# A decoder step on one core: weight sums moved beside the scores, left factors ordered and pooled anew

## The chip, the cores and the metric

The program runs on one core of a Trainium2 chip. The metric is the device time of one launch in microseconds, the median over several runs; lower is better. The core has five engines that each work through their own list of instructions in order: TensorE (PE in the profile; PEld is its weight load), VectorE (DVE), ScalarE (ACT), GpSimd (POOL) and SyncE (SP). In this kernel SP issues every DMA.

## The reference

One layer of a decoder for 2048 prompt tokens and 64 sample tokens, width 1024, all in fp32: a mixer of mLSTM heads and a convolution module, cross-attention into 256 memory tokens, then a ConvFFN. Cut to the parts that the change touches:

```python
qx = (hc @ w['x_wq']).reshape(B, L, X_HEADS, X_HEAD_DIM)
sc = jnp.einsum('blhd,bmhd->bhlm', qx, mem_k) * (X_HEAD_DIM ** -0.5)     # scores
pr = jax.nn.softmax(sc, axis=-1)
ox = jnp.einsum('bhlm,bmhd->blhd', pr, mem_v).reshape(B, L, D_MODEL)
x = x + ox @ w['x_wo']                                                   # output rows
hf = rmsnorm(x, w['norm_ffn'])
uf = hf @ w['f_wup']                                                     # (tokens,1024)@(1024,5632)
fa, fg = uf[..., :D_FF], uf[..., D_FF:]
fa_c = causal_dwconv(f_ext, w['f_conv_w'], w['f_conv_b'])                # width 3
x = x + (jax.nn.gelu(fa_c) * fg) @ w['f_wdown']                          # (tokens,2816)@(2816,1024)
y = rmsnorm(x, norm_final)
```

## The kernel before, in words

Every fp32 operand of a product is split into a high part (an ACT cast to fp32r) and a low part (a DVE or POOL subtraction): `split`. A product is then three matmuls: `mm3`. The large products are taken as 2 by 2 blocks with seven products in place of eight, named B11, B21, B22, T1, T2, T3, T4. Each needs a left and a right factor, which are blocks or sums of blocks.

The stages that matter here, by their place in the span: the *folds* (to 990 us) multiply `x_wq` into the memory keys and so make seven sets of right factors. `put` splits some tiles of them straight into `wf0` to `wf6`; the rest goes to DRAM (`wfd`) and comes back through `load_factors`. *Scores* (991 to 1186): eight pairs of 128-row token tiles. A pair is loaded and normed (`pair_in`), transposed and summed to left factors (`pair_sums`: four POOL sums `a<-a` among them), and split into seven left tiles `l` (`pair_split`); then come the seven products. Two of the seven left tiles lie in pool `pa`; the other five lie in `ap`, a pool that opens once the fold pool `fms` is closed, in the same space. *Output rows* (1186 to 1425) do the same with the probabilities and with seven factor sets `mo`.

*FFN up* (1441 to 2426): three blocks of 6, 5 and 5 token tiles. `rows_in` loads and norms a block's rows in two halves, `block_input` transposes them and makes seven right operands `R0` to `R6`, and 11 steps over weight pairs follow (`raw<-in_f_wup`, sums, splits into `wt`). The first block's rows are loaded, both halves, before `block_input` is entered. The left factors of the next stage are stored to DRAM as `l_d`.

*Down-projection* (2441 to 2899): for each of the seven products (B11, B21, T2, T3, T1, B22, T4) eleven right tiles `ws` (`wt` or `w`) and eight left factors, j = 0 to 7: `left_factor` loads `lr` (704 KB), splits it into `l` and 33 matmuls run, one unit. The residual rows `acc` are loaded beside the first two products. `weight_sums(k)`, once for each k of 11, is called beside units 1 to 11: it loads two tiles of `f_wdown` (`wr`, 512 KB each), multiplies them with the sample rows (`psG<-wr,ysr`), makes the four sums, two on DVE and two on POOL, and stores them as `ds`, from where the right factors T1 to T4 are read back.

All of `xt`, `raw` (of factor sets), `wr` and the probabilities share one ring of six tiles (pool `xw`). A scheduler sets each engine's order from the program order and its estimates.

Of the kernel before, what the change touches and what calls it, by code (L numbers as in the profile page):

```python
# [45 lines left out]
L_BUFS = 2, 6  # L46
# [42 lines left out]
R_ORDER = 1, 2, 3, 0, 4, 5, 6  # L89
# [4 lines left out]
def trunk_kernel(ctx: ExitStack, tc: tile.TileContext, i: dict, o: list):  # L94
# [1002 lines left out]
    def fold_keys(pools, mT, ps_, tps_):  # L1097
# [363 lines left out]
    def rows_in(blk, junk=None):  # L1461

        t0, nt_, smp = blk
        hc = nt_ * P // 2
        halves = []
        for z in range(2):
            xts = []
            first, n = t0 * P + z * hc, hc + (HS if smp else 0)
            for c0 in range(0, n, P):
                nt = min(P, n - c0)  # L1470
                t = xw.tile([P, D], F32, name="xt", tag="xt")
                c = c0
                while c < c0 + nt:
                    if c < hc:
                        tid, r0 = divmod(first + c, P)
                        m = min(P - r0, c0 + nt - c, hc - c)
                    else:
                        tid, r0, m = NT, z * HS, HS
                    SY.dma_start(t[c - c0:c - c0 + m], x2_d[tid][r0:r0 + m])
                    c += m  # L1480
                norm_x([(t, nt)], junk() if junk else fe_.tile([P, D], BF16, name="junk", tag="junk"), V)
                xts.append((t, nt))
            halves.append(xts)
        return halves
# [126 lines left out]

    pas = ExitStack()
# [97 lines left out]
    def block_input(blk, rows):  # L1710
# [118 lines left out]
    wdn = i["f_wdown"][0]  # L1829
# [7 lines left out]
    R_next = block_input(C_BLOCKS[0], ahead)  # L1837
    for bi, (t0, nt_, smp) in enumerate(C_BLOCKS):
# [84 lines left out]
    lp = ctx.enter_context(tc.tile_pool(name="lp", bufs=2, side="right", reuse_waits="tile"))  # L1923
# [35 lines left out]

    sums_d = [[dram(f"ds{kh}_{k}", [P, 2, 512]) for k in range(FP)] for kh in range(2)]  # L1960
# [4 lines left out]
    def weight_sums(k):  # L1965

        r = []
        for kh in range(2):
            t = xw.tile([P, 2, 512], F32, name="wr", tag="xt")
            SY.dma_start(t, wdn[(2 * k + kh) * P:(2 * k + kh + 1) * P, :].rearrange("p (c d) -> p c d", c=2))  # L1970
            for c in range(2):
                mm(pts[c * S:(c + 1) * S], ysr[:, 2 * k + kh], t[:, c], k + kh == 0, k + kh == FP)
            r.append(t)
        (b11, b12), (b21, b22) = [[t[:, c] for c in range(2)] for t in r]
        tt(b22, b22, b12, ALU.subtract)
        tt(b12, b12, b11, ALU.subtract, G)
        tt(b11, b11, b22, ALU.add)
# [126 lines left out]
```

## Time and profile before

| | |
|---|---|
| runs | 2911.03, 2922.74 (median), 2926.61 us |
| profiled execution | 2908.07 us, its span 2906.3 us |
| PE busy | 2721.0 us, 94% |
| DVE / ACT / POOL busy | 70% / 48% / 41% |
| DMA | 520.39 MB, mean 179 GB/s |

Busy time is the time in which an engine executed; PEclk is the granted clock of TensorE as a share of full speed (1.00 is 2.4 GHz). The span is the profiled execution from its first to its last instruction; 1.8 us of the execution's time lie outside it.

### The profile page before, as it was taken

What the parts mean: (1) busy time and instruction counts of PE and PEld (TensorE: products, weight loads), DVE (VectorE), ACT (ScalarE), POOL (GpSimd) and SP (SyncE); (2) the same over time, 40 slices, a digit from 0 to 9 for tenths busy, and PEclk for the clock granted to TensorE, in tenths of its full rate; (3) what the DMA queues carried; (4) which work ended last, traced back from release to release, by engine and by line L of the source; (5) the groups of instructions that cost most, each with busy time, mean ns of one, the idle gap of its engine ahead of it and who ended that gap; (6) DMA issues with size and microseconds to landing.
All of it is one profiled execution on the core that took longest, in us unless ns stands there. A gap on an engine that the chain in (4) does not pass through costs nothing. (4 is left out here: it accounts for less than half of the span.)

```text
span 2906.3 us, 44255 instructions
## 1 busy us (share of the span) xinstructions
PE 2721.0 (94%) x15768; PEld 2395.9 (82%) x15768; DVE 2042.0 (70%) x3395; ACT 1397.4 (48%) x2777; POOL 1195.4 (41%) x1285
## 2 busy tenths in 40 slices
PE   7999999989989799999799999999999997999998
PEld 6889989976768688666689988899989996678887
DVE  4588898793234678653599999888888885454454
ACT  4576678783232475412463334744454452232233
POOL 1558555461210442533464544554464442213200
PEclk9999999998999899999899999999999998999999
DMA  7635423354576632757645555666656567994454
GB/s 187 198 116 184 129 77 112 107 167 157 181 235 229 228 102 98 243 203 257 201 141 187 169 183 172 179 200 196 197 171 189 169 187 214 329 297 134 135 169 132
DMA packets 433317, 520.39 MB, mean 179 GB/s; under 512 B 61917, under 2 KB 331971, under 8 KB 433088
## 3 DMA queue, kind: packets, MB, share of 16 engines
q1 hardware_dynamic: 433096, 517.56, 56.0%
q8 instruction: 124, 2.03, 0.3%
q14 instruction: 97, 0.79, 0.1%
HBM read 352.18 MB, written 165.65 MB: 178 GB/s over the span
## 5 line engine op out<-in xcount | busy, mean ns | idle before, releaser
L294 ACT CAST wt<-raw 128x512 fp32r<-128x512 f32 x510 | 306.1, 617 | 309.9 <-DVE raw L125 68.4
L125 DVE TENSOR_TENSOR wt<-raw,wt 128x512 fp32r<-128x512 f32 x358 | 321.2, 902 | 45.8 <-ACT wt L294 45.2
L125 POOL TENSOR_TENSOR cside<-cside,cprod 128x512 f32<-128x512 f32 (+2 forms) x248 | 250.4, 1010 | 121.1 <-ACT cprod L117 91.1
L125 POOL TENSOR_TENSOR wt<-raw,wt 128x512 fp32r<-128x512 f32 x152 | 226.0, 1488 | 131.4 <-ACT wt L294 125.7
L122 DVE SCALAR_TENSOR_TENSOR psG<-ue,vc,psG 128x512 f32<-128x512 f32 (+2 forms) x448 | 256.5, 572 | 22.2 <-ACT psG L117 13.3
L148 PE MATMUL psA<-R,wt 128*128 128x384 f32 (+2 forms) x1392 | 246.3, 328 | 5.4 <-DVE u L125 2.6
L148 PEld LDWEIGHTS psA<-R,wt 128*128 128x128 f32 x1392 | 229.4, 191 | 8.1 <-ACT wt L294 3.2
L294 ACT CAST l<-lr 128x1408 fp32r<-128x1408 f32 x56 | 77.0, 1376 | 283.3 <-PE psA L148 67.7
L117 ACT ACTIVATE cprod<-ue,vc 128x512 f32<-128x512 f32 (+2 forms) x248 | 146.6, 604 | 28.2 <-POOL cside L125 20.3
L125 DVE TENSOR_TENSOR l<-lr,l 128x1408 fp32r<-128x1408 f32 x56 | 98.6, 1761 | 67.0 <-ACT l L294 59.3
L122 DVE SCALAR_TENSOR_TENSOR y<-fe,vc,y 128x640 f32<-128x640 f32 (+1 forms) x132 | 134.5, 1052 | 5.4 <-ACT y L117 5.3
L148 PE MATMUL psA<-wf,l 128*128 128x512 f32 x516 | 132.7, 400 | 4.9 <-DVE b L129 1.9
L148 PE MATMUL psG<-R,wt 128*128 128x320 f32 (+2 forms) x696 | 128.3, 327 | 4.6 <-DVE fe L125 2.5
L148 PE MATMUL psD<-R,wt 128*128 128x320 f32 (+2 forms) x696 | 127.8, 328 | 4.8 <-DVE u L125 3.4
L125 POOL TENSOR_TENSOR y<-y,u 128x384 f32<-128x384 f32 (+2 forms) x66 | 80.4, 1218 | 125.5 <-ACT wt L294 51.7
L148 PE MATMUL psE<-R,wt 128*128 128x352 f32 (+2 forms) x696 | 126.3, 324 | 5.7 <-DVE u L125 4.5
L148 PE MATMUL psF<-R,wt 128*128 128x352 f32 (+2 forms) x696 | 126.6, 325 | 3.0 <-DVE fe L125 2.2
L148 PE MATMUL psC<-R,wt 128*128 128x384 f32 (+2 forms) x684 | 121.9, 323 | 7.7 <-DVE u L125 7.7
L148 PE MATMUL psB<-R,wt 128*128 128x384 f32 (+2 forms) x684 | 124.2, 326 | 1.7 <-DVE fe L125 1.5
L148 PE MATMUL psD<-h,wt 128*128 128x256 f32 (+1 forms) x768 | 117.6, 298 | 7.0 <-DMA h<-h 5.3
L141 POOL TENSOR_TENSOR r<-v,nhalf 128x1 f32<-128x1 f32 (+1 forms) x63 | 40.0, 640 | 203.5 <-DVE v L131 201.1
L148 PEld LDWEIGHTS psD<-R,wt 128*128 128x128 f32 x696 | 115.0, 191 | 8.2 <-ACT wt L294 3.2
(662 smaller groups left out, 6934.0 us busy)
## 6 DMA issues: line engine op xcount, KB each, us to landing
raw<-in_f_wup SPq DMA_DIRECT2D x88, 512.0 KB
raw<-sum SPq DMA_DIRECT2D x88, 512.0 KB
lr<-l SPq DMA_DIRECT2D x49, 704.0 KB
sum<-raw SPq DMA_DIRECT2D x44, 512.0 KB
xt<-x SPq DMA_DIRECT2D x42, 512.0 KB
xt<-in_x_prompt SPq DMA_DIRECT2D x32, 512.0 KB
x<-xt SPq DMA_DIRECT2D x32, 512.0 KB
h<-h SPq DMA_DIRECT2D x56, 256.0 KB
```

The source lines that it names most:

```text
L117: A.activation(out, in_, func, bias=bias, scale=scale)
L122: V.scalar_tensor_tensor(out=out, in0=in0, scalar=s, in1=in1, op0=op0, op1=op1)
L125: (eng or V).tensor_tensor(out=out, in0=a, in1=b, op=op)
L141: G.tensor_tensor(out=y, in0=v, in1=e.to_broadcast(sh), op=ALU.pow)
L148: T.matmul(out, lhsT, rhs, start=start, stop=stop)
L294: A.copy(hi, src)
```

## The change

Four edits. (1) `weight_sums` is called beside the scores (pairs 0 to 7) and the output rows (pairs 0 to 2), with all four sums on POOL; the sample rows' product reads `f_wdown` again, a tile for each of 22 units from B21 on (`sample_rows`), and its result is added after T3. (2) Scores: six left tiles lie in a new pool `pl`, and the sixth factor set lies in `ap` beside the seventh left tile; T4's factor tiles all go through DRAM. (3) FFN up: the first block's second half of rows is loaded inside `block_input`; the `R` tiles are allocated in another order, the weight `raw` tiles have a pool of their own, the carry tiles come later. (4) Down: the raw left factors of units 0 and 1 are loaded early into the `xw` ring, unit 0's is split into three `wt` tiles, each later one is loaded two units ahead, and the second half of `acc` is placed beside T2.

```diff
-L_BUFS = 2, 6
+L_BUFS = 6, 2
+ACC_AT = 0, 2
+WF_ORDER = 1, 2, 5, 4, 3, 0
...
-            if dst is None:
+            if dst is None or q == T4:
                 SY.dma_start(wf_d[q][:, k], x)
...
+    def weight_sums(k):
+        r = []
+        for kh in range(2):
+            t = xw.tile([P, 2, 512], F32, name="wr", tag="xt")
+            SY.dma_start(t, wdn[(2 * k + kh) * P:(2 * k + kh + 1) * P, :].rearrange("p (c d) -> p c d", c=2))
+            r.append(t)
+        (b11, b12), (b21, b22) = [[t[:, c] for c in range(2)] for t in r]
+        tt(b22, b22, b12, ALU.subtract, G)
+        tt(b12, b12, b11, ALU.subtract, G)
+        tt(b11, b11, b22, ALU.add, G)
+        tt(b21, b21, b11, ALU.subtract, G)
+        for kh in range(2):
+            SY.dma_start(sums_d[kh][k], r[kh])
...
     nxt += pair_split(sums0, range(L_BUFS[0], 7))
+    wf.append(factor_6())
+    load_factor(wf[6], wf_d[6], KT // 2)
...
             scores(scp, p, left, lambda: next(side) if p + 1 == NT // 2 else None)
+            weight_sums(p)
...
+            if p < FP - NT // 2:
+                weight_sums(NT // 2 + p)
...
-    ahead = rows_in(C_BLOCKS[0], junk_rows)
+    ahead = rows_in(C_BLOCKS[0], 0, junk_rows)
...
+        xts1 = rows[1] if len(rows) > 1 else rows_in(blk, 1, lambda: junk)
...
+    def sample_rows(f):
+        t = xw.tile([P, 2, 512], F32, name="ws", tag="xt")
+        SY.dma_start(t, wdn[f * P:(f + 1) * P, :].rearrange("p (c d) -> p c d", c=2))
+        for c in range(2):
+            mm(pts[c * S:(c + 1) * S], ysr[:, f], t[:, c], f == 0, f == FT - 1)
...
+    with tc.high_priority():
+        ahead = [left_raw(B11, j, True) for j in range(2)]
+    first = left_first(ahead.pop(0))
...
-            l = left_factor(q, j)
-            if qi < 2:
-                accs[qi].append(acc_rows(qi, j))
+            l = left_factor(ahead.pop(0)) if qi + j else first
+            n_ = qi * NJ + j + 2
+            if n_ < len(ORDER) * NJ:
+                ahead.append(left_raw(ORDER[n_ // NJ], n_ % NJ))
+            if qi in ACC_AT:
+                accs[ACC_AT.index(qi)].append(acc_rows(ACC_AT.index(qi), j))
...
-            if qi < 2 and 0 < qi * NJ + j <= FP:
-                weight_sums(qi * NJ + j - 1)
+            if 0 <= (qi - 1) * NJ + j < FT:
+                sample_rows((qi - 1) * NJ + j)
```

Where the order moves, first SP's at the start of the scores. `wfd` are factor tiles in DRAM (the number ending in 40 is T4), `xt<-x` the rows of the pairs, `ds` the weight sums, `p` the probabilities. Before:

```order
L1658 DMA raw<-wfd_10040 128x1024 [waits DMAHW7_49,DVE_49]
L1658 DMA raw<-wfd_10040 128x512 [waits DMAHW6_49,Pool_49]
L1425 DMA xt<-x_2_171 128x1024 [waits DMAHW1_49,DVE_49]
L1425 DMA xt<-x_3_172 128x1024 [waits DMAHW3_49,DVE_49]
L1425 DMA xt<-x_4_173 128x1024 [waits DMAHW0_49,Pool_49]
L1425 DMA xt<-x_5_174 128x1024 [waits DMAHW5_49,DVE_49]
L1425 DMA xt<-x_6_175 128x1024 [waits DMAHW2_49,Pool_49]
L1425 DMA xt<-x_7_176 128x1024 [waits DMAHW4_49,Pool_49]
L1425 DMA xt<-x_8_177 128x1024 [waits DVE_49,PE_49]
L1437 DMA p_10041<-sc 128x512 [waits DVE_49]
```

After:

```order
L1685 DMA raw<-wfd_10040 128x1024 [waits DMAHW4_49,Pool_49]
L1130 DMA wfd_10040<-b 128x512 [waits Pool_49]
L1685 DMA raw<-wfd_10040 128x1024 [waits DMAHW6_49,DMAHW5_49]
L1427 DMA xt<-x_2_171 128x1024 [waits DMAHW1_49,DVE_49]
L1427 DMA xt<-x_3_172 128x1024 [waits DMAHW0_49]
L1619 DMA wr<-in_f_wdown 128x1024 [waits DMAHW2_49,DVE_49,Activation_49]
L1619 DMA wr<-in_f_wdown 128x1024 [waits DMAHW3_49,DVE_49]
L1427 DMA xt<-x_4_173 128x1024 [waits DMAHW4_49,DVE_49,Pool_49]
L1427 DMA xt<-x_5_174 128x1024 [waits DMAHW6_49,DVE_49,Pool_49]
L1619 DMA wr<-in_f_wdown 128x1024 [waits DVE_49,PE_49]
L1439 DMA p_10041<-sc 128x512 [waits DVE_49]
L1627 DMA ds_0_10057<-wr 128x1024 [waits DMAHW7_49,DMAHW1_49,Pool_49]
```

T4's last tile is now written and read back ahead of pair 1's rows, and between the rows of one pair and the next stand the `wr` loads and `ds` stores, the latter behind a wait for POOL.

Next ACT's order at the start of FFN up. `b<-psB` is the first transposed feature of the block, `junk,ss<-xt` and `xt<-xt,r` are a row tile's squares and its scaling. Before:

```order
L294 CAST wt<-raw 128x512 [waits PE_49]
L294 CAST wt<-raw 128x512 [waits DVE_49]
L294 CAST wt<-raw 128x512 [waits Pool_49]
L294 CAST wt<-raw 128x512 x2
L294 CAST wt<-raw 128x512 [waits DMAHW3_49]
L294 CAST wt<-raw 128x512 [waits DMAHW6_49]
L294 CAST wt<-raw 128x512
L119 ACTIVATE junk,ss<-xt 128x1024 [waits DMAHW7_49]
L117 ACTIVATE xt<-xt,r 128x1024 [waits DMAHW4_49,Activation_49,Pool_49]
L119 ACTIVATE junk,ss<-xt 128x1024 [waits DMAHW2_49]
L117 ACTIVATE b<-psB,vc_432 128x384
L117 ACTIVATE b<-psC,vc_432 128x384
```

After:

```order
L296 CAST wt<-raw 128x512 [waits DMAHW7_49]
L296 CAST wt<-raw 128x512
L119 ACTIVATE b<-psB,vc_432 128x384 [waits PE_49]
L119 ACTIVATE b<-psC,vc_432 128x384 [waits PE_49]
L121 ACTIVATE junk,ss<-xt 128x1024 [waits DMAHW6_49,PE_49]
L296 CAST R_15523<-b 128x384 [waits Activation_49] x2
L119 ACTIVATE b<-psB,vc_432 128x384 [waits PE_49]
L119 ACTIVATE b<-psC,vc_432 128x384 [waits PE_49]
L296 CAST wt<-raw 128x512 [waits DVE_49]
L296 CAST wt<-raw 128x512 [waits Pool_49]
L296 CAST wt<-raw 128x512 x2
L296 CAST wt<-raw 128x512 [waits DMAHW0_49]
```

The first features now stand behind two weight casts, not behind eight casts and two tiles' squares and scaling; the other casts follow two features later.

Last SP's order at the start of the down-projection, from the last store of the stage ahead (`l<-ls`). `lr<-l` are raw left factors, of rows of 128 or 64 tokens. Before:

```order
L1905 DMA l_15367<-ls 128x4x320 [waits DMAHW0_49,Pool_49]
L2003 DMA lr<-l_15365 128x11x128 [waits DMAHW1_49]
L1955 DMA acc<-x_0_186 128x1024 [waits DMAHW2_49,PE_49]
L2056 DMA ysr<-ys 128x1408 [waits DMAHW7_49,DMAHW5_49,DMAHW3_49]
L2059 DMA accs<-x_16_202 64x512 [waits DMAHW4_49]
L2059 DMA accs<-x_16_202 64x512
L2003 DMA lr<-l_15365 128x11x128 [waits DMAHW6_49]
L1955 DMA acc<-x_1_187 128x1024 [waits PE_49]
L1955 DMA acc<-x_2_188 128x1024 [waits DMAHW0_49]
L1955 DMA acc<-x_6_192 128x1024 [waits DMAHW1_49]
L1970 DMA wr<-in_f_wdown 128x1024 [waits DMAHW2_49,DVE_49]
L1955 DMA acc<-x_7_193 128x1024 [waits DMAHW3_49]
```

After, from the same store, and then the piece that ends with unit 5's factor (two halves of 64 rows):

```order
L1939 DMA l_15473<-ls 128x4x320 [waits DMAHW6_49,Pool_49]
L2030 DMA lr<-l_15471 128x11x128 [waits DMAHW7_49,PE_49]
L1989 DMA acc<-x_0_186 128x1024 [waits DMAHW0_49,PE_49]
L2109 DMA ysr<-ys 128x1408 [waits DMAHW5_49,DMAHW3_49,DMAHW1_49]
L2112 DMA accs<-x_16_202 64x512 [waits DMAHW2_49]
L2112 DMA accs<-x_16_202 64x512
L2030 DMA lr<-l_15472 128x11x128 [waits DMAHW4_49]
L1989 DMA acc<-x_1_187 128x1024
L1989 DMA acc<-x_2_188 128x1024 [waits DMAHW6_49]
L1989 DMA acc<-x_6_192 128x1024 [waits DMAHW7_49]
L1989 DMA acc<-x_7_193 128x1024 [waits DMAHW0_49]
L1989 DMA acc<-x_8_194 64x1024 [waits DMAHW1_49]
```

```order
L2015 DMA wr<-in_f_wdown 128x512 [waits DMAHW1_49]
L2000 DMA ws<-in_f_wdown 128x1024 [waits DMAHW2_49]
L1989 DMA acc<-x_3_189 128x1024 [waits DMAHW3_49]
L1989 DMA acc<-x_4_190 128x1024 [waits DMAHW4_49]
L1989 DMA acc<-x_5_191 128x1024 [waits DMAHW5_49]
L1989 DMA acc<-x_8_194 64x1024 [waits DMAHW6_49]
L1989 DMA acc<-x_9_195 64x1024 [waits DMAHW7_49]
L1989 DMA acc<-x_9_195 64x1024 [waits DMAHW0_49,PE_49]
L2030 DMA lr<-l_15472 128x11x64 [waits DMAHW1_49,DVE_49]
L2030 DMA lr<-l_15473 128x11x64 [waits DMAHW2_49]
```

The loads for units 0 and 1 have moved some 170 rows ahead of this place, so the first `lr` here is unit 2's. Unit 4's load stands four rows behind the first of these two pieces, and 19 other loads stand between it and unit 5's.

## Rows read from the trace of the kernel before

**Rows 1.** The page's first part: busy time, share of the span, instructions of each engine.

```profile
PE 2721.0 (94%) x15768; PEld 2395.9 (82%) x15768; DVE 2042.0 (70%) x3395; ACT 1397.4 (48%) x2777; POOL 1195.4 (41%) x1285
```

**Rows 2.** Windows: from:to, length, busy time (instructions) by engine, PEclk, DMA share, GB/s.

```profile
980.00:1017.00 37.00, 18.15 (x104) 15.41 (x103) 31.55 (x32) 23.82 (x44) 29.31 (x24) 0.77 0.65 216
1017.00:1190.00 173.00, 170.41 (x809) 137.89 (x807) 135.67 (x277) 111.13 (x271) 54.07 (x56) 0.99 0.34 112
1190.00:1425.00 235.00, 230.34 (x1218) 159.91 (x1216) 115.61 (x164) 70.55 (x128) 104.17 (x94) 1.00 0.66 232
1425.00:1475.00 50.00, 28.39 (x123) 22.99 (x123) 35.54 (x54) 34.86 (x64) 25.75 (x28) 0.73 0.61 189
1475.00:1805.00 330.00, 306.77 (x1728) 301.16 (x1728) 322.66 (x398) 134.82 (x219) 169.43 (x153) 0.99 0.53 173
2426.50:2600.00 173.50, 153.74 (x623) 106.93 (x621) 77.67 (x92) 45.00 (x55) 37.68 (x26) 0.93 0.99 311
2600.00:2870.00 270.00, 270.00 (x1193) 223.58 (x1192) 137.26 (x147) 84.94 (x101) 51.74 (x35) 1.00 0.54 157
```

**Rows 3.** PE's waits from 930 to 1480: total, times, longest, in us.

```profile
PE psB L145 <- ACT b L117: 17.9, 2, 16.5
PE psG L148 <- ACT l L294: 16.6, 1, 16.6
```

**Rows 4.** PE in order of time, scores' start: start, us, operation [idle before <- releaser].

```profile
994.54 3.01 PE L148 MATMUL psA<-wf,l 128*128 128x512 f32 x12 [0.38 <-DVE b L129]
1014.12 1.22 PE L148 MATMUL psG<-wf,l 128*128 128x512 f32 x2 [16.57 <-ACT l L294]
...
1034.64 2.88 PE L148 MATMUL psG<-wf,l 128*128 128x512 f32 x12
```

**Rows 5.** ACT in order of time at the start of FFN up.

```profile
1425.06 0.62 ACT L294 CAST wt<-raw 128x512 fp32r<-128x512 f32 x1 [4.40 <-PE psA L148]
1432.15 3.73 ACT L294 CAST wt<-raw 128x512 fp32r<-128x512 f32 x7 [6.48 <-DVE raw L125]
1435.94 1.06 ACT L119 ACTIVATE junk<-xt 128x1024 bf16<-128x1024 f32 x1
...
1439.87 1.04 ACT L119 ACTIVATE junk<-xt 128x1024 bf16<-128x1024 f32 x1
...
1440.91 0.56 ACT L117 ACTIVATE b<-psB,vc 128x384 f32<-128x384 f32 x1
```

**Rows 6.** PE in order of time at the start of the down-projection.

```profile
2441.34 1.22 PE L148 MATMUL psA<-wt,l 128*128 128x512 f32 x2 [14.57 <-ACT l L294]
...
2477.07 0.73 PE L148 MATMUL psA<-wt,l 128*128 128x512 f32 x2 [2.58 <-ACT l L294]
2478.73 9.42 PE L148 MATMUL psA<-wt,l 128*128 128x512 f32 x28 [0.93 <-DVE l L125]
...
2488.67 6.96 PE L148 MATMUL psD<-wt,l 128*128 128x512 f32 x30
```

**Rows 7.** ACT in order of time there: the cast of the first left factor.

```profile
2439.92 1.36 ACT L294 CAST l<-lr 128x1408 fp32r<-128x1408 f32 x1 [12.36 <-DMA lr<-l]
```

**Rows 8.** SP's DMA issues in order of time there.

```profile
2433.22 0.57 SPq L2003 DMA_DIRECT2D lr<-l  x1
```

**Rows 9.** POOL's costliest group from 1017 to 1190, forms apart.

```profile
L125 POOL TENSOR_TENSOR a<-a 128x512 f32<-128x512 f32 x32 | 41.5, 1315 | 57.8 <-ACT a L1401 44.2 <-DVE s L1382 12.9
```

**Rows 10.** DVE's groups of the same stretch.

```profile
L125 DVE TENSOR_TENSOR l<-a,l 128x512 fp32r<-128x512 f32 x58 | 40.9, 736 | 6.4 <-ACT l L294 6.2
L129 DVE TENSOR_SCALAR sc<-sc,s 128x256 f32<-128x256 f32 x64 | 30.9, 524 | 0.9
...
L129 DVE TENSOR_SCALAR s<-s 128x2 f32<-128x2 f32 x32 | 8.2, 286 | 0.1
```

**Rows 11.** Tiles s and sc of the same stretch: ns min/median/max, first and last start.

```profile
L129 DVE TENSOR_SCALAR sc<-sc,s x64: 336/352/1451, 1025.1 to 1185.2; 128x256 f32<-128x256 f32 x64
...
L129 DVE TENSOR_SCALAR s<-s x32: 145/159/1251, 1019.2 to 1181.5; 128x2 f32<-128x2 f32 x32
```

More of the change, by code (lines that the diff above doesn't have):

```diff
@@ L1459, in out_rows, with rows_in @@
             SY.dma_start(x2_d[t], xt)
-    def rows_in(blk, junk=None):
+    def rows_in(blk, z, junk=None):
         t0, nt_, smp = blk
         hc = nt_ * P // 2
[L1465 to L1484, printed above, removed]
+        xts = []
+        first, n = t0 * P + z * hc, hc + (HS if smp else 0)
+        for c0 in range(0, n, P):
+            nt = min(P, n - c0)
+            t = xw.tile([P, D], F32, name="xt", tag="xt")
+            c = c0
+            while c < c0 + nt:
+                if c < hc:
+                    tid, r0 = divmod(first + c, P)
+                    m = min(P - r0, c0 + nt - c, hc - c)
+                else:
+                    tid, r0, m = NT, z * HS, HS
+                SY.dma_start(t[c - c0:c - c0 + m], x2_d[tid][r0:r0 + m])
+                c += m
+            norm_x([(t, nt)], junk() if junk else fe_.tile([P, D], BF16, name="junk", tag="junk"), V)
+            xts.append((t, nt))
+        return xts
     def own_tiles(pp):
@@ L1698, in trunk_kernel @@
     wtp = ctx.enter_context(tc.tile_pool(name="wtf", bufs=WT_BUFS, side="right", reuse_waits="tile"))
+    rawf = us.enter_context(tc.tile_pool(name="rawf", bufs=RAW_BUFS, side="right", reuse_waits="tile"))
     f2 = us.enter_context(tc.tile_pool(name="f2", bufs=2, side="right", reuse_waits="tile"))
@@ L1727, in put @@
             split(R[q][:, 0, k, :n], R[q][:, 1, k, :n], x, gain, eng)
-        xts, xts1 = rows
+        xts = rows[0]
         half = range(KT // 2)
         b11, t3 = [btile() for _ in half], [utile(n) for _ in half]
+        junk = fe_.tile([P, D], BF16, name="junk", tag="junk")
         for q in R_ORDER:
@@ L1836, in trunk_kernel @@
     wa_next = load_pair(0, True)
-    R_next = block_input(C_BLOCKS[0], ahead)
+    R_next = block_input(C_BLOCKS[0], [ahead])
+    carry = fe_.tile([P, FT, 2], F32, name="carry")
+    G.memset(carry, 0.0)
+    fst = fe_.tile([P, FT, 2 * NB], F32, name="fst")
+    cy_s = fe_.tile([P, FT, 2 * NB], F32, name="cy_s")
     for bi, (t0, nt_, smp) in enumerate(C_BLOCKS):
@@ L1919, in trunk_kernel @@
     us.close()
-    lp = ctx.enter_context(tc.tile_pool(name="lp", bufs=2, side="right", reuse_waits="tile"))
+    lp = ctx.enter_context(tc.tile_pool(name="lp", bufs=1, side="right", reuse_waits="tile"))
     dp = ctx.enter_context(tc.tile_pool(name="dp", bufs=1, reuse_waits="tile"))
@@ L1963, in trunk_kernel @@
     w_turn = cycle([wtile] * WT_BUFS + [lambda: dp.tile([P, 2, 512], F32R, name="w", tag="w", bufs=DW_BUFS)] * DW_BUFS)
[L1965 to L1977, printed above, removed]
-        tt(b21, b21, b11, ALU.subtract, G)
-        for kh in range(2):
-            SY.dma_start(sums_d[kh][k], r[kh])
+    def sample_rows(f):
[3 more added lines that the diff above has]
+            mm(pts[c * S:(c + 1) * S], ysr[:, f], t[:, c], f == 0, f == FT - 1)
     def right_factors_down(q):
@@ L2016, in out_rows_norm @@
         out_norm(accs[z][j], P, [(y_prompt[0, t0:t0 + m], r, m) for t0, m, r in token_rows(z, j)])
+    l_side = cycle((1, 0))
+    l_room = [lp.tile([P, 2, FP, P], F32R, name=f"l{z}", tag=f"l{z}") for z in range(2)]
     accs = [], []
-    for qi, q in enumerate((B11, B21, T2, T3, T1, B22, T4)):
+    ORDER = B11, B21, T2, T3, T1, B22, T4
+    with tc.high_priority():
+        ahead = [left_raw(B11, j, True) for j in range(2)]
+    first = left_first(ahead.pop(0))
+    for qi, q in enumerate(ORDER):
         ws = right_factors_down(q)
```

84 lines of the change are left out of this document (53 added, 31 removed).

## The prediction

> **What bounds the kernel now.** I read the page's first part, then the windows by stage, then PE's waits, then the orders in time around the three longest waits. TensorE is busy 94% of the span [rows 1], so the question is where it isn't. The windows [rows 2] show two kinds of stretch. In the scores (1017 to 1190) and the steady part of the down-projection (2600 to 2870) PE is busy for nearly every microsecond; in FFN up's first block (1475 to 1805) DVE is, 322.66 of 330 us, and PE follows. Between the stages stand three holes. PE's waits [rows 3] name two of them: 16.6 us for a left tile `l` at the start of the scores, 16.5 us for a feature `b` at the start of FFN up. The third, 14.57 us, opens the down-projection [rows 6]. Around each hole the granted clock is below full (2.4 GHz): 0.77 in 980 to 1017, 0.73 in 1425 to 1475, 0.93 in 2426.5 to 2600. The change touches these three, and pays with work put beside the scores. I sum against the profiled execution's own 2908.07 us, which is 14.67 us below the median of 2922.74.
>
> **Scores' start, -4 us.** PE has two products done by 997.55 and then waits for the third [rows 4], whose left tile lies in a pool that opens only when the folds' buffers are free. With six left tiles in a pool of their own that wait goes. Next late are the factors: T4's last tile now goes to DRAM and back, and pair 1's rows `xt<-x_2`, `x_3` are queued on SP behind that read. The store waits for POOL's last fold sum, and the folds' last splits, too, are what the old wait ended on (an ACT cast behind them released PE at 1014.12). So pair 0's products may run early, but all seven now stand ahead of pair 1's transposes, and its rows come later. I place pair 1's third product at about 1030.5 instead of 1034.64: 4 us, an estimate between its bounds. They are 10 us gained (the hole of 16.57 less some 6.5 us for T4's way to DRAM and back, for which the nearest row is a factor's 6.7 us from issue to cast, 2433.22 to 2439.92 in [rows 7, 8]), and 4 us lost if pair 1's rows arrive at the old hole's end and still have their norm ahead of them.
>
> **FFN up's start, -8 us.** Before, ACT casts seven weight tiles at 1432.15 after 6.48 us of waiting for DVE's weight sums, then squares and scales two row tiles, and only then copies the first feature, at 1440.91 [rows 5]. Afterwards that copy stands directly behind two casts of which the second started at 1425.06. PE then starts near 1427, does the first two features, and stands again when ACT reaches the cast that waits for DVE's sums (1432.15 before). The second half's rows are loaded later and must still be normed in the block. I expect the first product's end about 10 us sooner, of which the DVE-bound block gives on only what DVE had idle: in 1425 to 1475 DVE is busy 35.54 of 50, so 14.5 us can be regained at most, and 8 is my value. Bounds: 13 (the hole less some 3 us from `b` to the first product) and 0 (DVE's work in the block is the same; if its first work comes no sooner, nothing is won).
>
> **Down-projection's start, -12 us.** In 2600 to 2870 a matmul takes 270.00 / 1193 = 0.226 us, a unit of 33 takes 7.47 us. In 2426.5 to 2600 there are 623, worth 141.0 us, in 173.5 us: 32.5 us are lost [rows 2]. They are the hole of 14.57, a second wait of 2.58 and 0.93 us before unit 3, and units run at a lower clock: unit 3 takes 2477.07 to 2488.67 = 11.6 us [rows 6]. The DMA share there is 0.99 at 311 GB/s: the queue is full, and unit 0's factor, issued at 2433.22 [rows 8], was cast at 2439.92 [rows 7]. Afterwards units 0 and 1 are loaded before the stage, so the first hole shrinks to the split's own time; some DVE splits of right tiles stand ahead of it, so I leave 3 us. The queue stays. Behind the last store `l<-ls` the new order has, up to and with unit 5's factor, four `lr` of 704 KB, 6400 KB of `acc`, `ysr` 704, `accs` 256, `nf` 512, nine `wr` of 256 and one `ws` of 512: 13,504 KB or 13.8 MB, 44.5 us at 311 GB/s from 2433.2. Unit 5 then lands at 2477.7 and is split some 3 us later (cast 1.36 and the DVE part), at 2480.5, whereas PE, started at 2429.5, wants it at 2429.5 + 5 x 7.47 = 2467. So a wait of about 13 us opens before unit 5; with 4 us of low clock behind it (unit 3 lost 11.6 - 7.5 before) the loss is 3 + 13 + 4 = 20, and the gain 32.5 - 20 = 12. Bounds: 28 (the queue runs faster, no wait before unit 5, 3 + 1.5 us left) and 0 (a rate of 240 GB/s: it lands at 2491 and the wait is 27). What leaves the stage besides, 22 sums on DVE and 22 on POOL, and 11.5 MB in DMA that comes in from B21 on (22 `ws` loads of 512 KB, against 157 GB/s used in 2600 to 2870), lies beside PE at no cost: DVE is busy 137 of 270 us there, the DMA share is 0.54. That cover is gone only if a unit's DVE work comes near the unit's 7.47 us; it would then cost what exceeds it. The sample matmuls move, they do not go.
>
> **What is put beside the scores, +6 us.** Eight calls bring 32 POOL sums of 1.315 us [rows 9], 42 us on top of 54.07 in 173: POOL is no bound, at 96. Three calls beside the output rows bring 16 us to 104.17 of 235. But some DVE instructions run long there: `sc` takes 352 ns at the median and up to 1451, `s` 159 and up to 1251 [rows 11]. Against its median, `sc` is busy 30.9 - 64 x 0.352 = 8.4 us too long, `s` 8.2 - 32 x 0.159 = 3.1 [rows 10], together 11.5 us, which I put down to POOL's 32 sums: 0.36 each. Thus 32 more cost DVE some 12 us, 135.67 becomes 148 of 173, and PE, busy 170.41, sees a part of it where a softmax or a split is late: between 0 and 12, I take 3, as DVE keeps 25 us of room. The other 3 us are for SP: the stores `ds` wait for POOL, and the next pair's rows, loaded three pairs ahead before, are queued behind them, with two of the ring's six tiles held. Bounds for both together: 0 and 20. Code that issues more (44 DMAs on SP; at the 0.57 us of [rows 8] 25 us in 400) lies beside the rest: no cost of its own.
>
> A rule speaks against this part. The Trainium skill ("SBUF — State Buffer", Who interferes with whom) says that a DVE instruction with two SBUF inputs, or a tensor_scalar in a mode that uses two ports, and a GpSimd instruction that reads SBUF exclude each other, for the whole instruction. By that alone 32 sums could hold DVE for 42 us; 135.67 + 42 = 178 is more than the 173 us, and the scores would be at least 5 us longer, the sum 5 us less favourable. The trace agrees that one waits (an `sc` of 352 ns took up to 1451, [rows 11]) but with 0.36 us for each sum, not 1.3, so I keep 12.
>
> **Sum.** -4 - 8 - 12 + 6 = -18: 2890 against 2908.07, which against the median is 2922.74 - 18 = 2904.7.
>
> **Rivals.** *All three holes close.* For it: each is one named wait, not a share of a busy engine. Against it: the queue at 0.99 and the DVE-bound block. It gives -10 - 13 - 28 + 3 = -48, 2875.
>
> *The waits only change their names.* The factors' round trip holds pair 1, block 0 stays bound by DVE, and unit 5 takes over unit 0's hole. For it: 322.66 of 330 us on DVE, and 13.8 MB ahead of unit 5. Against it: all three together are needed for it, and units 0 to 4 run early in any case. It gives -2 - 2 - 3 + 6 = about 0, 2922.
>
> *SP's queue holds up the scores: slower.* One mechanism: a pair's rows stand behind a store that waits for four POOL sums. A pair has 173 / 8 = 21.6 us; its chain is load, norm, transposes, four POOL left sums (5.3 us), splits. The weight sums take 5.3 us of the same engine, and where they stand before the left sums PE waits for these. It decides as soon as rows are loaded less than one pair ahead. Price: 5.3 us in each of 11 calls, 58 us, less the 24 us gained at the starts: +34, 2957; with half the calls exposed +5 to +10, which is no change. For it: the order's two `ds` stores between pairs. Against it: POOL is idle two thirds of the scores.
>
> **Chances.** The forecast 0.50, all holes close 0.20, waits renamed 0.18, slower 0.12. The likeliest one's own range is 2892 to 2917. The range of 8 in 10 reaches from 2870 (the full gain with a little more) to 2936 (the costs at 20 and the gains at half); left out are a full gain with no cost beside the scores and most of the slower case. About 0.5%, 14.6 us, is what a measurement of this kernel can tell from no change. The forecast of -18 falls beyond that in seven cases of ten: faster 0.50 x 0.7 + 0.20 = 0.55, slower 0.12, the same 0.33.
>
> **What would show it.** Scores' start: the wait of `psG` for `l` gone, pair 1's third product at 1030 to 1031; later than 1034 shows that the round trip took it back. FFN up: the first `b<-psB` near 1427, a wait of some 6 us after the second feature, and the block, from the output rows' last product to its end, 8 us shorter; if it is as long as before, DVE was the bound. Down: PE at work within 4 us of the last up matmul, and a wait before `psE` of unit 5 of about 13 us for `lr`; if that wait is absent the full gain holds, if it exceeds 20 the stage gains nothing. Scores and output rows: PE's busy share in the middle of both as before; a wait for `xt<-x` or for POOL `a` of 4 us or more in each pair shows the slower rival.

## The result and the profile after

The changed kernel takes 2950.98 us (median of four runs, 2949.24 to 2954.9), the kernel before 2920.69 beside it: 1.0119 times as long, 95% interval 1.0099 to 1.0138. It is 30 us slower where 18 us less were forecast, outside the range of 2870 to 2936.

The page's first part, to be held against [rows 1], and the windows of the changed kernel by stage (columns as in [rows 2]): first score products, pairs 1 to 7, output rows, FFN up's start and first block, first product of the down-projection.

```profile
PE 2750.1 (93%) x15768; PEld 2412.3 (82%) x15768; DVE 2038.2 (69%) x3375; ACT 1399.2 (47%) x2780; POOL 1223.3 (42%) x1308
```

```profile
993.60:1026.50 32.90, 26.66 (x102) 20.40 (x102) 31.36 (x34) 18.89 (x38) 22.37 (x18) 0.86 0.57 201
1026.50:1205.90 179.40, 160.76 (x740) 129.27 (x740) 138.41 (x262) 109.28 (x265) 93.62 (x88) 0.95 0.55 189
1205.90:1460.90 255.00, 240.39 (x1228) 165.86 (x1229) 115.25 (x165) 72.90 (x132) 123.45 (x110) 0.97 0.71 249
1460.90:1851.40 390.50, 350.61 (x1900) 338.03 (x1898) 372.05 (x465) 176.58 (x293) 202.68 (x187) 0.94 0.53 174
2465.00:2555.00 90.00, 69.53 (x280) 52.52 (x278) 31.90 (x42) 23.51 (x32) 3.25 (x3) 0.89 0.91 254
```

PE has the same 15768 instructions and is busy 29 us longer, so part of the loss is matmuls at a lower clock; the clock is below 1.00 in every one of these stretches, where [rows 2] has 0.99 and 1.00 in scores and output rows. From the first matmul of each stage in the order in time (PE's last instruction is at 2898.6 before and 2939.7 after):

| stage | before, us | after, us | difference | forecast |
|---|---|---|---|---|
| up to the first score product | 991.2 | 993.6 | +2.4 | 0 |
| to pair 1's first product | 39.9 | 33.0 | -6.9 | -4 |
| pairs 1 to 7 | 154.2 | 179.4 | +25.2 | +6 (both rows) |
| output rows | 239.8 | 255.0 | +15.2 | |
| FFN up: start | 17.7 | 6.0 | -11.7 | -8 (both rows) |
| FFN up: block 0 | 374.0 | 384.5 | +10.5 | |
| FFN up: blocks 1, 2 | 609.6 | 613.5 | +3.9 | 0 |
| down-projection | 472.3 | 474.8 | +2.5 | -12 |

The two waits of [rows 3] are gone and others have come. PE's waits of the changed kernel from the scores to the start of the output rows, then at the start of the down-projection:

```profile
PE psA L150 <- ACT wf L296: 6.9, 2, 5.2
PE psB L147 <- ACT a L1403: 6.7, 1, 6.7
PE psA L150 <- DVE u L127: 6.1, 2, 5.2
```

```profile
PE psE L150 <- ACT l L296: 12.2, 1, 12.2
PE psD L150 <- ACT l L296: 5.7, 1, 5.7
```

Three of these waits can be followed, the one for `u` first. In the order of time, POOL, then DVE, then PE around 1100 us of the changed kernel:

```profile
1096.23 5.27 POOL L127 TENSOR_TENSOR a<-a 128x512 f32<-128x512 f32 x4 [2.22 <-ACT a L1403]
...
1103.68 4.96 POOL L127 TENSOR_TENSOR wr<-wr 128x512 f32<-128x512 f32 x3
```

```profile
1099.15 2.50 DVE L131 TENSOR_SCALAR sc<-sc,s 128x256 f32<-128x256 f32 x2
...
1105.01 1.90 DVE L131 TENSOR_SCALAR sc<-sc,s 128x256 f32<-128x256 f32 x2
1106.83 2.95 DVE L127 TENSOR_TENSOR l<-a,l 128x512 fp32r<-128x512 f32 x3
...
1110.91 1.40 DVE L127 TENSOR_TENSOR u<-u,psA 128x512 f32<-128x512 f32 x2
```

```profile
1103.53 2.98 PE L150 MATMUL psF<-wf,l 128*128 128x512 f32 x12
1111.73 3.75 PE L150 MATMUL psA<-wf,l 128*128 128x512 f32 x8 [5.22 <-DVE u L127]
```

POOL runs four left sums `a` and then weight sums `wr`. Beside them two scalings `sc` at a time take 2.50 and 1.90 us on DVE, where two take 0.7 at the median of [rows 11]; the additions `u`, which empty PSUM banks, follow late in DVE's order, and PE stands 5.22 us. The clock falls behind it, and pair 4 takes 28.4 us where a pair takes 20.8: 7.6 for a wait of 5.2. The second wait, for `a`, is in pair 1 and of another kind: ACT copies `a` behind the squares of pair 3's first row tile, for which it waits:

```profile
1040.50 1.06 ACT L121 ACTIVATE junk<-xt 128x1024 bf16<-128x1024 f32 x1 [4.30 <-DMA xt<-x]
...
1042.54 0.56 ACT L1403 COPY a<-psB 128x512 f32<-128x512 f32 x1
```

The third, 5.2 us for a factor tile `wf`, stands at the end of pair 7, ahead of the first product of the output rows.

### The profile page after: what moved, and what is told of

It reads as the page before. It is cut to its first block, busy times and chain, and to the rows that moved or that the text cites. A ratio compares the mean times of both kernels' runs of the same rounds, so it can differ in the third digit from the quotient of the medians.

```text
span 2947.5 us, 44276 instructions
## 1 busy us (share of the span) xinstructions
PE 2750.1 (93%) x15768; PEld 2412.3 (82%) x15768; DVE 2038.2 (69%) x3375; ACT 1399.2 (47%) x2780; POOL 1223.3 (42%) x1308
## 5 line engine op out<-in xcount | busy, mean ns | idle before, releaser
L150 PE MATMUL psA<-R,wt 128*128 128x384 f32 (+2 forms) x1392 | 252.3, 332 | 17.4 <-DVE xt L127 5.4
L150 PEld LDWEIGHTS psA<-R,wt 128*128 128x128 f32 x1392 | 232.8, 194 | 22.4 <-DVE R L127 6.7
L296 ACT CAST l<-lr 128x1408 fp32r<-128x1408 f32 (+2 forms) x56 | 75.6, 1352 | 267.4 <-PE psA L150 75.2
L150 PE MATMUL psA<-wf,l 128*128 128x512 f32 x516 | 139.3, 414 | 19.6 <-ACT wf L296 6.9
L127 POOL TENSOR_TENSOR acc<-acc,c 128x512 f32<-128x512 f32 x24 | 43.6, 1831 | 255.7 <-DVE c L127 246.3
L150 PEld LDWEIGHTS psA<-wf,l 128*128 128x128 f32 x516 | 99.1, 198 | 52.0 <-issue 11.8
L127 DVE TENSOR_TENSOR l<-lr,l 128x1408 fp32r<-128x1408 f32 (+2 forms) x56 | 97.6, 1744 | 61.9 <-ACT l L296 61.0
L150 PEld LDWEIGHTS psC<-R,wt 128*128 128x128 f32 x684 | 114.8, 193 | 11.3 <-issue 10.1
```

The lines of the kernel that those rows point to most:

```text
L127: (eng or V).tensor_tensor(out=out, in0=a, in1=b, op=op)
L150: T.matmul(out, lhsT, rhs, start=start, stop=stop)
L296: A.copy(hi, src)
```

## The experiments

Theory A is that POOL's sums cost, by stretching DVE's instructions beside them; theory B, the slower rival of the prediction, that the ring and SP's queue cost, by bringing rows and factors late; theory C that edits 2 to 4 cost. Stage times of all runs, in us:

| run | to score | start | pairs 1 to 7 | output rows | up: start + block 0 | down |
|---|---|---|---|---|---|---|
| before | 991.2 | 39.9 | 154.2 | 239.8 | 391.7 | 472.3 |
| changed | 993.6 | 33.0 | 179.4 | 255.0 | 390.5 | 474.8 |
| undo_sums | 993.4 | 36.7 | 160.9 | 236.9 | 389.8 | 476.8 |
| sums_alone | 994.6 | 40.0 | 174.0 | 253.0 | 390.9 | 477.8 |
| no_pool_sums | 995.4 | 32.7 | 167.5 | 244.7 | 390.0 | 471.8 |
| own_tiles | 993.8 | 33.3 | 182.1 | 252.4 | 388.6 | 472.5 |
| memset_sums | 986.6 | 33.4 | 173.0 | 243.9 | 388.6 | 473.2 |
| scratch_sums | 993.5 | 32.8 | 176.1 | 254.6 | 387.2 | 472.2 |
| acc_late | 1000.4 | 32.5 | 177.1 | 253.3 | 390.2 | 458.7 |
| sums_in_folds | 1006.8 | 35.2 | 165.5 | 238.0 | 391.4 | 470.4 |
| folds_acc_late | 1005.0 | 35.1 | 166.5 | 237.1 | 389.0 | 457.8 |
| folds_old_pools | 1004.7 | 42.4 | 154.2 | 240.6 | 386.4 | 455.5 |
| down_sums_acc_late | 989.8 | 41.1 | 154.2 | 239.3 | 390.2 | 461.7 |

Runs with the same code up to the scores differ there by up to 14 us (986.6 to 1000.4), so single profiles are compared stage by stage and totals by their ratios to the kernel before that ran beside them.

The stage "pairs 1 to 7" must be read pair by pair. From the first matmul of a pair to that of the next one (every pair has 84; pair 7 ends at the first product of the output rows), in us:

| run | pair 1 | 2 | 3 | 4 | 5 | 6 | 7 |
|---|---|---|---|---|---|---|---|
| before | 21.7 | 20.8 | 20.8 | 20.8 | 20.8 | 20.8 | 28.4 |
| undo_sums | 28.4 | 20.8 | 20.8 | 20.8 | 20.8 | 20.8 | 28.4 |
| sums_in_folds | 32.9 | 20.9 | 20.8 | 20.8 | 20.8 | 20.8 | 28.4 |
| folds_acc_late | 33.9 | 20.9 | 20.8 | 20.8 | 20.8 | 20.8 | 28.4 |
| no_pool_sums | 30.3 | 21.6 | 21.4 | 20.8 | 20.8 | 20.8 | 31.7 |
| memset_sums | 32.8 | 21.6 | 21.9 | 22.0 | 20.9 | 20.8 | 33.0 |
| changed | 33.6 | 21.8 | 21.6 | 28.4 | 20.9 | 20.8 | 32.4 |
| scratch_sums | 31.7 | 23.2 | 26.5 | 20.9 | 20.8 | 20.8 | 32.1 |
| own_tiles | 33.2 | 20.9 | 28.2 | 20.8 | 21.8 | 28.8 | 28.4 |
| sums_alone | 27.1 | 20.8 | 22.1 | 24.8 | 24.7 | 22.6 | 31.9 |

The 25.2 us of the changed kernel are 11.9 in pair 1, 7.6 in pair 4, 4.0 in pair 7 and 1.9 in the others. Pair 1 is long in every run with edit 2, also where nothing is put beside the scores (undo_sums and the two runs with the sums in the folds).

**Edit 1 taken back, and edit 1 alone.** In the first, `weight_sums` is called as before; the second is the kernel before with only this moved:

```diff
-            weight_sums(p)
...
-            if 0 <= (qi - 1) * NJ + j < FT:
-                sample_rows((qi - 1) * NJ + j)
+            if qi < 2 and 0 < qi * NJ + j <= FP:
+                weight_sums(qi * NJ + j - 1)
```

> The changed kernel with the weight sums back beside units 1 to 11 of the down-projection, as before; edits 2 to 4 stay. If the sums beside the scores and output rows are what costs (changed kernel: first score product to last output-row product 467.4 us, before 433.9), that stretch falls to about 427 (433.9 less the 6.9 us won at the scores' start), FFN up stays within 2 us of before, and the time is 2906 to 2914, that is 7 to 15 us under before. If instead edits 2 to 4 are what costs (left tiles and factor set in other pools), the stretch stays above 455 and the time above 2940.

> The kernel before with edit 1 alone: weight sums beside scores and output rows, sample rows from B21 on. If the sums are what costs: the stretch from the first score product to the last output-row product is 470 to 475 us (433.9 plus the 40 us that the changed kernel loses after pair 1), the first product of the down-projection is shorter by 10 to 20 us as less DMA stands there, and the time is 2940 to 2955. If edits 2 to 4 are what costs: within 10 us of 2921.

Taken back: 2920.18 us, ratio to before 1.0024 (1.0009 to 1.0039). Alone: 2951.17, 1.0129 (1.0102 to 1.0157). Edit 1 alone is as slow as the whole change, so it is the cause, and theory C falls as the account of the loss. But taking it back leaves no gain of 7 to 15 us: edits 2 to 4 together cost some 7 us instead, and scores and output rows take 434.5 us where 427 were expected. By edit 1 alone pairs 1 to 7 are 19.8 us longer and the output rows 13.2, together 33.0; the stretch from the first score product on is 467.0 us, just under the 470 to 475 expected. The first product of the down-projection, which it was to shorten by 10 to 20 us, takes 96.2 us instead of 101.0, and the whole stage 5.5 more.

**The sums left out; the tiles out of the ring.**

```diff
-        tt(b22, b22, b12, ALU.subtract, G)
-        tt(b12, b12, b11, ALU.subtract, G)
-        tt(b11, b11, b22, ALU.add, G)
-        tt(b21, b21, b11, ALU.subtract, G)
```

```diff
-            t = xw.tile([P, 2, 512], F32, name="wr", tag="xt")
+            t = wsp.tile([P, 2, 512], F32, name="wr", tag="wr", bufs=2) if wsp else xw.tile([P, 2, 512], F32, name="wr", tag="xt")
...
-            weight_sums(p)
+            weight_sums(p, scp)
```

> The changed kernel without the four subtractions and additions of each weight sum: the tiles are loaded into the ring and stored as they are, so the factors T1 to T4 of the down-projection are not the reference's. All 44 DMAs and the ring tiles stay; POOL has 44 operations less and the stores wait for no engine. Theory A (POOL's sums stretch DVE's instructions and hold POOL's left sums and SP's stores): the stretch falls from 467 to 430 to 440, the time to 2915 to 2925. Theory B (ring tiles and SP's queue, so rows and factors arrive late): the stretch stays at 455 or more, the time at 2940 or more.

> The changed kernel with the weight tiles of the eight calls beside the scores in two tiles of their own, not in the ring of six; the three calls beside the output rows stay in the ring. SP's order then has pair rows three pairs ahead again. POOL does the same sums. Theory B (ring and queue): pair 1 to first output-row product falls from 179.4 us to 160 or less (before 154.2), the time to about 2930. Theory A (DVE and POOL): that stretch stays at 172 or more, the time at 2943 or more.

Without the sums: 2919.3 us, 1.0022 (1.0006 to 1.0038), as theory A has it, though the stretch from the first score product on is 444.9 us, above its 430 to 440. With own tiles: 2944.25, 1.0111 (1.0083 to 1.0138); pairs 1 to 7 take 182.1 us, no less than in the changed kernel, with rows loaded three pairs ahead again. The total is theory A's, but it hides two things. PE waits twice for `u`, not once, in pairs 3 and 6; and the wait for `wf` at the end of pair 7 is 1.23 us:

```profile
1089.81 3.50 PE L150 MATMUL psE<-wf,l 128*128 128x512 f32 x8 [5.70 <-DVE u L127]
...
1160.91 3.75 PE L150 MATMUL psG<-wf,l 128*128 128x512 f32 x8 [5.99 <-DVE u L127]
...
1209.14 0.50 PE L150 MATMUL psA<-wf,l 128*128 128x512 f32 x1 [1.23 <-ACT wf L296]
```

Without the sums, but with the tiles in the ring, that last wait is still 4.56 us. So the ring does cost, 4 us in pair 7: a part of theory B holds.

Of the 36.6 us by which pairs and output rows are longer than with edit 1 taken back (434.4 against 397.8), the sums are 22.2 (434.4 - 412.2) and 14.4 stay with loads and stores alone. Of these 14.4, 7.8 lie in the output rows and 3.3 in pair 7; 1.9 lie in pair 1, whose length varies more than that without any load beside it.

**What of POOL's work does it: memset in place of sums, and sums that no store waits for.**

```diff
+        for t in r:
+            for c in range(2):
+                G.memset(t, 0.0)
```

```diff
+            for x, y, op in ((b22, b12, ALU.subtract), (b12, b11, ALU.subtract), (b11, b22, ALU.add), (b21, b11, ALU.subtract)):
+                tt(pool.tile([P, 512], F32, name="dst", tag="dst"), x, y, op, G)
```

> The changed kernel with each of the four POOL sums of a call replaced by a POOL memset of a whole weight tile, so T1 to T4 are not the reference's. POOL still does work before each store and SP still waits for it, but POOL reads nothing from SBUF. If POOL's reading is what stretches DVE (two operands against one port): DVE's excess beside the scores falls from 30.0 us to about 15 (as without the sums), pair 1 to first output-row product from 179.4 to 168 to 171, the time to 2918 to 2928. If POOL's time and the stores behind it are what costs: DVE's excess may fall but the stretch stays at 176 or more and the time at 2940 or more. A memset may well be shorter than a sum; its duration is read from the run.

> The changed kernel; in the eight calls beside the scores POOL writes its four sums to a scratch tile, and the weight tiles are stored as they were loaded, so the stores wait for no engine (the factors T1 to T4 of these calls are not the reference's). POOL's work is the same 42 us, SP is free of it. If SP's stores waiting for POOL are what makes the scores longer: pair 1 to first output-row product falls from 179.4 to 170 or less and the time to 2942 or less. If POOL's time beside DVE is: it stays at 175 to 182, the time within 5 us of 2951.

Memset: 2927.92 us, 1.0056 (1.0038 to 1.0073), pairs 1 to 7 at 173.0, between the two cases expected. Scratch: 2940.06, 1.0102 (1.0083 to 1.0121), pairs 1 to 7 at 176.1, as expected of POOL's time; the total is 11 us under 2951, but the kernel before took 2910.59 beside it. SP's stores no longer wait in the pairs, and most of the loss there stays: the stores are not it. With memsets the pairs are shorter, but DVE's stretch did not fall by half as expected. The groups of DVE and POOL in pairs 1 to 7 (columns as in [rows 10]): two fences for the changed kernel, one without sums, two with memsets, one with scratch:

```profile
L127 DVE TENSOR_TENSOR l<-a,l 128x512 fp32r<-128x512 f32 x56 | 41.5, 773 | 11.4 <-ACT l L296 11.4
L131 DVE TENSOR_SCALAR sc<-sc,s 128x256 f32<-128x256 f32 x64 | 40.3, 670 | 0.9
...
L1384 DVE RECIPROCAL s<-s 128x2 f32<-128x2 f32 x31 | 5.0, 162 | 22.4 <-ACT sc L121 22.4
```

```profile
L127 POOL TENSOR_TENSOR wr<-wr 128x512 f32<-128x512 f32 x30 | 42.0, 1399 | 33.9 <-issue 19.2 <-DMA wr<-in_f_wdown 9.5 <-PE psA L150 2.5
```

```profile
L127 DVE TENSOR_TENSOR l<-a,l 128x512 fp32r<-128x512 f32 x56 | 38.9, 723 | 6.0 <-ACT l L296 5.9
L131 DVE TENSOR_SCALAR sc<-sc,s 128x256 f32<-128x256 f32 x64 | 29.2, 498 | 0.9
```

```profile
L131 DVE TENSOR_SCALAR sc<-sc,s 128x256 f32<-128x256 f32 x64 | 39.5, 658 | 1.0
L127 DVE TENSOR_TENSOR l<-a,l 128x512 fp32r<-128x512 f32 x56 | 37.4, 702 | 11.6 <-ACT l L296 11.5
```

```profile
L1624 POOL MEMSET wr<- 128x1024 f32 x30 | 28.5, 958 | 28.9 <-DMA wr<-in_f_wdown 13.8 <-PE psE L150 13.1 <-issue 1.4
```

```profile
L127 DVE TENSOR_TENSOR l<-a,l 128x512 fp32r<-128x512 f32 x56 | 46.1, 853 | 15.3 <-ACT l L296 15.2
L131 DVE TENSOR_SCALAR sc<-sc,s 128x256 f32<-128x256 f32 x64 | 37.6, 630 | 0.9
```

The same 64 scalings `sc` take 29.2 us without the sums, 40.3 with them, 39.5 beside memsets; the 56 subtractions `l`, which read two operands, take 38.9, 41.5 and 37.4. So a POOL operation that only writes stretches the scaling, and not the subtraction. The Trainium skill ("SBUF — State Buffer", Who interferes with whom) says just that: a tensor_scalar in a two-port mode contends with any GpSimd operation, an operation with two SBUF inputs only with one that reads SBUF. The rows agree, for a scaling in such a mode; in which mode it ran no row shows.

What PE loses does not follow the sum of these stretches. DVE is busy 124.2 us in the pairs without the sums, 134.3 with memsets, 138.4 in the changed kernel and 144.3 with scratch; the pairs take 167.5, 173.0, 179.4 and 176.1. The loss comes in single waits of PE for `u` or `l` from DVE: 5.2 us in the changed kernel, 5.7, 6.0 and 0.7 with own tiles, 2.3, 1.3, 0.8 and 0.7 with scratch, up to 2.1 with edit 1 alone, 0.6 at most with memsets, and none over 0.6 with edit 1 taken back or without the sums. Where such a wait falls differs from run to run; pairs 5 and 6 of the changed kernel are not longer at all.

**The queue of the down-projection.** One column of each `acc` tile is written first by POOL, from a result of two units before, so that the load can't be ordered earlier:

```diff
         t = dp.tile([P, D], F32, name="acc", tag=f"acc{z}_{j}")
+        if z or j > 1:
+            G.tensor_copy(t[:, :1], accs[0][j][:, :1] if z else cs[j - 2][:, :1])
```

> The changed kernel, down-projection only: a one-column POOL copy into each acc tile ties its load to the unit two before (second half: to the unit of B21), so the scheduler can't pull the acc loads ahead. From the last store to unit 5's factor stand 9664 KB instead of 13,504. If the waits before units 4 and 5 (5.7 and 12.2 us in the changed kernel) are the queue's: they fall to about 2 and 5 us, the down-projection from 474.8 to 460 to 464, the time to 2936 to 2940. If they are not the queue's order but DMA throughput or DVE: the waits stay and the time is within 4 us of 2951.

2934.1 us, 1.0069 (1.0052 to 1.0086) where the changed kernel has 1.0119: 0.0050 or 14.6 us less, and the down-projection takes 458.7, a little less than the 460 to 464 expected. PE's waits there, first of the changed kernel in order of time and then of this one:

```profile
2503.71 1.22 PE L150 MATMUL psD<-wt,l 128*128 128x512 f32 x2 [5.68 <-ACT l L296]
...
2527.47 1.22 PE L150 MATMUL psE<-wt,l 128*128 128x512 f32 x2 [12.20 <-ACT l L296]
```

```profile
PE psA L150 <- ACT l L296: 3.2, 1, 3.2
PE psA L150 <- DVE w L127: 1.2, 2, 0.9
```

Both long waits are gone and one of 3.2 us, before unit 3, is left, so they were the order of the queue.

**Other places for the sums.** First one call behind each of eleven output parts of the stage ahead of the scores; then with `acc` held back; then with edit 2 undone as well; last, with edit 2 undone and `acc` held back, with the sums back in the down-projection, beside units 3 to 13:

```diff
             out_part(outs.pop(0))
+            next_sums()
```

```diff
+            if qi < 2 and 2 < qi * NJ + j <= FP + 2:
+                weight_sums(qi * NJ + j - 3)
```

> The changed kernel with the eleven weight_sums calls moved from the scores and output rows to the stage before them (650 to 990 us, where DVE is busy 37% and POOL 19%); the sums themselves are the same, on POOL and in the ring. If contention for DVE and POOL beside the scores is the cause, pair 1 to first output-row product falls from 179.4 to 161 and the output rows from 255 to 237, as without the sums; the folds get 0 to 10 us longer; the time is 2915 to 2925. If the sums cost wherever they are put (DMA, ring), the time stays above 2940.

> Both at once: weight sums in the folds and acc loads held back. If the two costs are separate, they add: 2902 to 2912, under the kernel before (2915 to 2921) by 5 to 15 us. If the gains overlap or the folds pay, 2915 or more.

> Weight sums in the folds and acc loads held back, edit 2 undone (left tiles and factor sets as before, seven factors together); edits 3 and 4 stay. The scores' start goes back to 39.9 us and pair 1 to its 21.7 us: start plus pairs 194 us instead of the 201.6 of the run with edit 2. If edit 2 costs what its stages say, the time is 4 to 8 us under that run's 2913: 2905 to 2909, and 5 to 10 us under the kernel before. If the early start of the scores is worth something after all, it is 2913 or more.

> Edit 2 undone as well, and the weight sums back in the down-projection, beside units 3 to 13, two on DVE and two on POOL, with the acc loads held back; edits 3 and 4 stay. Nothing is put beside the folds (they cost 12 us) or the scores. If the DMA queue of the first two products has room for the sums once acc has left it, the down-projection takes 462 to 468 us (472.3 before, 476.8 with the sums there and acc early) and the time is 2900 to 2908, 7 to 15 us under before. If the queue is full anyway, it takes 474 or more and the time is within 4 us of before.

In the folds: 2927.98 us, 1.0051 (1.0037 to 1.0066), missed by 3 us, as the stage ahead of the scores pays some 12 (1004.7 to 1006.8 us in the three runs with the sums there, 986.6 to 1000.4 in those with edit 2 and no sums there); pairs 1 to 7 take 165.5 where 161 were expected, by pair 1. PE waits there for a cast `ct`, 9.0 us in one place, where the kernel before has four such waits of 2.7 at most:

```profile
PE psD L150 <- ACT ct L296: 12.7, 5, 9.0
```

With `acc` late: 2913.15, 1.0005 (0.9992 to 1.0018), 1 us over what was expected: the two costs add, but the sum is no gain. With edit 2 undone: 2913.97, 1.0003 (0.9988 to 1.0018); pairs 1 to 7 fall to 154.2, but the start is 42.4, and the expected 4 to 8 us were not there. With the sums in the down-projection: 2900.79 against 2910.59, 0.9974 (0.9962 to 0.9985), as expected, and the only version faster than the kernel before. The page's first part and its longest waits at the start of the down-projection:

```profile
PE 2725.2 (94%) x15768; PEld 2396.3 (83%) x15768; DVE 2042.2 (71%) x3398; ACT 1395.3 (48%) x2780; POOL 1200.6 (41%) x1299
```

```profile
PE psB L150 <- ACT wt L296: 4.0, 1, 4.0
PE psD L150 <- ACT l L296: 1.0, 1, 1.0
```

The first two products take the sums' DMA once `acc` has left the queue: nothing waits longer than 4.0 us.

## Why the prediction was wrong

**The step that failed** is the cost of what is put beside the scores and output rows: +6 forecast, with a bound of 20; edit 1 alone measured +33.0, and taking it out of the changed kernel frees 36.6. (The +40.4 of the stage table holds besides what edit 2 does to pair 1.) Three terms were mis-sized.

The first is the cover: of the stretch on DVE, PE "sees a part of it where a softmax or a split is late", 3 us, "as DVE keeps 25 us of room". The size on DVE was nearly right: 0.36 us for each sum made 12 us, and DVE is busy 138.4 us in pairs 1 to 7 against 124.2 without the sums, 14 more. But DVE's room is no reserve at the right place: it waits 22.4 us for ACT's `sc` and 11.4 for ACT's `l` in the changed kernel, inside the chain of softmax, splits and PSUM additions of each pair. Where the stretch fell on the links ahead of `u`, PE stood, and each wait of 5 to 6 us cost about 2 more at a lower clock. That PE lost 11.9 us (179.4 - 167.5) for 14 on DVE is chance: 7.6 of it lie in pair 4 behind one wait, 3.3 in pair 1, which varies from 28.4 to 33.9 us without any sum beside it, and 0.7 in pair 7.

The second is the output rows, which got no price of their own: they are 18.1 us longer than with edit 1 taken back, 10.3 by the sums and 7.8 by loads and stores. For the sums it is not DVE, which is busy 115.3 us there and 119.2 without them. Pair 3 takes 38.0 us instead of 30.8, and so in the other runs with these sums (34.3 to 36.6); in the order of time of PE, POOL and SP:

```profile
1343.95 1.93 PE L150 MATMUL psE<-xt,own 128*32 128x256 f32 x32 [1.55 <-POOL own L1517]
...
1349.15 1.11 PE L147 MATMUL psB<-ident,xt 128*128 128x128 f32 x4 [2.90 <-DMA xt<-p]
```

```profile
1340.85 2.62 POOL L127 TENSOR_TENSOR wr<-wr 128x512 f32<-128x512 f32 x2 [12.06 <-DMA wr<-in_f_wdown]
1343.41 0.24 POOL L1517 COPY own<-pr 128x64 f32<-128x64 f32 x1
```

```profile
1344.64 0.33 SPq L1445 DMA_DIRECT2D xt<-p  x1
1345.07 0.37 SPq L1627 DMA_DIRECT2D ds<-wr  x1
```

POOL's copy `own` stands behind two weight sums, PE's product waits for it, and the load of the probabilities `p`, before which SP has waited 8.9 us for PE, lands late. It is issued ahead of the `ds` store, so here it is POOL's time and not the store. With memsets, which are shorter and have the stores as well, pair 3 takes 32.0 us and the output rows 243.9.

The third is the ring, priced within 3 us: 4 in pair 7.

**The rule I set aside** pointed the right way: by the exclusive port I worked out at least 5 us for the scores and kept 3. But it did so by a full DVE, and DVE was busy 138.4 us of 179.4; each sum cost it some 0.47 us, not 1.3.

**The slower rival** had about the right time (2957) by a mechanism that was the smaller part: the stores' wait for POOL is 3 us of it at most in the pairs (179.4 to 176.1), the ring 4, and no wait of 4 us or more stands in each pair.

**Scores' start**: pair 1's first product is 6.9 us nearer, beyond the 4 forecast, but the mark was set at its third product. The row at 1034.64 is by count its second; the third began at 1037.36 before and begins at 1044.78 now, behind the wait for `a`. By the prediction's own sign the gain was taken back. It is so without sums, too: with edit 2 and edit 1 taken back pair 1 takes 28.4 us instead of 21.7, so that start and pairs together are longer by 3.5 (197.6 against 194.1).

**FFN up's start**: the gap closed by 11.7, as read from ACT's order, and block 0 took 10.5 more. From output rows to block 0's end it is 391.7 before and 386 to 391 in the other runs: the lower bound, 0, was about the right end. DVE is busy 372 us of 390.5 there and 370 of 391.7 before, so it sets the block's end; this is read from its share, not tried.

**Down-projection**: PE went on at once, and the wait before unit 5 came as forecast (12.2 us, 13 expected), in part by luck: its factor was split 54.9 us behind the first `lr` after the last store, not 47.3, as the queue moved 250 to 300 GB/s there and not the 311 of the mean, and PE reached unit 5 late as well. A wait of 5.7 us before unit 4 was not seen. The sample rows' product cost more than its own time: a unit takes 7.48 us and one with four of these matmuls 8.72, some 0.33 more than four matmuls at the unit's rate, in all 7 us; the kernel before, with groups of eight (9.61 for such a unit), lost about half of that. In the prediction's terms the loss of 20 became 35: 2 at the start, 18 in two waits, 7 at a lower clock, 7 in these groups, 1 elsewhere. So -12 became +2.5.

**Open**: the 7.8 us that loads and stores cost the output rows without any sum, and why edit 2 makes pair 1 long. POOL's left sums `a` share the engine with the weight sums; in the wait followed above they came first, but no run keeps POOL's time and takes away DVE's stretch.

## What to carry to other kernels

An engine's idle share in a stage is no cover for work on its port partner: ask which link of the per-tile chain the stretched instruction is, and what stands behind the added work on its own engine. A stretch of 14 us on VectorE left most pairs untouched and cost 7.6 us in one, so read such a loss tile by tile, not as a stage's sum. Where a gap at a stage's start is closed, look at once for the engine that sets the stage's end, and in a full queue for the transfer that is late next: the order of the loads, not their sum, was worth 14 us here.

## What the runs showed of the hardware

A POOL memset, which reads nothing, lengthened VectorE's tensor_scalar as much as a sum did (39.5 and 40.3 us for 64, against 29.2) and left the two-operand subtraction alone (37.4 us for 56, against 38.9 without and 41.5 with sums). A wait of 5 to 6 us of TensorE made a pair of 20.8 us take 28 to 29, in the changed kernel and twice with own tiles, with a mean granted clock of 0.72 in the 12 us around the end of the wait (1108 to 1120) in the changed kernel; full speed, 2.4 GHz, was back in the next 12 us (1.00).
